# A streaming encoder layer: the third weight tile of attention requested sooner and cast later, other score tiles turned in gate banks, and the convolution behind the next sums

## The chip, the cores and the metric

The kernel runs on one core of a Trainium2 chip. The time is that of the device for one execution, in microseconds. PE multiplies matrices, ACT, DVE and POOL work elementwise, SP and POOL issue DMAs. Each engine runs its own row of instructions in order and waits for semaphores of the others.

## The reference

One layer over 1024 prompt rows and 32 sample rows of width 1024, in float32:

```
h = RMSNorm(x);  z = h @ W_in -> q_A, k_A, v_A, q_B, f_B, i_B, og_B, gate_A, gate_B
y_A = sliding-window attention (16 query heads, 2 kv heads of width 64, sinks, shared relative bias)
y_B = gated linear recurrence (8 heads), RMSNorm(o) * silu(og_B)
m = sigmoid(gate_A) * (y_A @ W_brA) + sigmoid(gate_B) * (y_B @ W_brB)
x = x + RMSNorm(m @ W_out)
[a | u] = RMSNorm(x) @ W_up;  a = causal depthwise conv3(a)
x = x + RMSNorm((gelu(a) * u) @ W_down)
x = x + (p @ W_ple) * sigmoid(x @ W_ple_gate)
```

A frame attends to its own chunk of 64 frames and the two before it.

## The kernel before, in words

**Products.** A float32 operand is split in two parts, a rounded high part and the rest, and a product is three matmuls: with `La`, `Lb` the high part and the rest of the input: `La` by `wh` (L203), `Lb` by `wh` (L204), `La` by `wl` (L205). A weight tile of 512 KB goes through three steps. `load_raw` asks for it (DMA at L173, on SP's queue) into one of two `wr` buffers. `load_next` casts it to the high part `wh` on ACT (L182), and DVE subtracts for the rest `wl` (L184). The plan of tiles is a list; `stream` takes one tile after the other, and keeps tiles ahead up to `limit[0]`.

**Attention.** The stage goes over eight head pairs i (two heads side by side). For each there are nine score tiles j: eight of 128 rows, and j = 8 with the 32 sample rows. `scores(i, j)` multiplies queries by keys (L498, L499), adds bias on DVE (L504), exponentiates on ACT (L509) and scales. `turn(i, j)` transposes the probabilities on PE (L535) into a PSUM bank, and splits them for the next product: ACT casts `ph` (L226), DVE subtracts for `pl` (L227). `values` multiplies them by the values (L554, L555) into a bank `o`, copied on ACT to `u` (L561) and added up on DVE to `ya` (L562, L563); the values of j = 8 go to the third quarter of its own turn's bank.

**What runs between them.** PE is filled with blocks of the projections: queries of the next pair and gates. `stream` counts half-blocks, m = 0, 1, 2 and so on, and `small[m]` lists what is put in behind half-block m: scores, turns, values, weight loads, bias loads. Gate and query blocks write `mm` banks, of which there are three; turns write `tr` banks, of which there are two, or in some cases an `mm` bank. A scheduler orders each engine's row by priority and readiness as it models them; `pinned(f, engines)` and `behind(engines)` hold an instruction behind the last one put on these engines so far. The reading of a finished gate block is a tanh on ACT (L295) and a store on SP (L296). `bias_load` and `bias_load8` fetch the bias of a pair and of its sample tile (L449, L460).

**The up projection.** For each unit f of 128 of the 2816 features, PE runs steps of 24 matmuls into banks X, Y and Z (L2001 to L2003), a scheme of block products from sums of operands. What comes out is combined behind the steps: s1 is copied on ACT (L2012), U2 = s1 - Y on DVE (L2014), L2016 writes a part of `ab`, nU3 = Y - s1 is L2019, L2021 and L2023 write the other factor `us`. L2014 and L2019 are the last readers of the bank Y, so a later step into Y waits for them. `ff_tail(f)` is a generator that runs in unit f + 1: copies at the ends of `ab` (L1937 to L1940), the convolution as one ACT instruction (L1941) and two multiply-adds on DVE (L1942, L1945), the gelu on ACT (L1946) and the product with `us` on DVE (L1947, L1948). Beside it weights are prepared from loaded tiles `wu`: POOL adds tiles (L1759, L1760, L1761, L1766), ACT casts (L1752) and DVE subtracts (L1753).

Of the kernel before, what the change touches and what calls it, by code (L numbers as in the profile page):

```python
# [14 lines left out]
ALU = mybir.AluOpType  # L15
# [44 lines left out]
def layer_kernel(  # L60
# [17 lines left out]
    def nm(s):  # L78
        n_names[0] += 1
        return f"{s}_{n_names[0]}"  # L80
# [5 lines left out]
    V, S, G, E = nc.vector, nc.scalar, nc.gpsimd, nc.tensor  # L86
# [69 lines left out]
    n_first = len(plan)  # L156
# [10 lines left out]
    limit = [n_first]  # L167
    raws, ready, used = [], [], [0]
# [54 lines left out]
    def split(hi, lo, src, scale=None):  # L223

        if scale is None:
            S.copy(hi, src)  # L226
            V.tensor_tensor(lo, src, hi.bitcast(F32), op=ALU.subtract)  # L227
        else:
            S.mul(hi, src, scale)
            V.scalar_tensor_tensor(lo, src, scale, hi.bitcast(F32), op0=ALU.mult, op1=ALU.subtract)  # L230

    def bank(pool, tag, bufs):
        return pool.tile([P, 512], F32, tag=tag, name=nm(tag), bufs=bufs)
# [4 lines left out]
    def mm_bank():  # L238
        return bank(pp, "mm", 3)

    def tr_bank():
        return bank(pp, "tr", 2)
# [35 lines left out]
    def unit(out):  # L278

        cell = []  # L280

        def get_w():
            if not cell:
                cell.append(next_w())
            return cell[0]
        return [(get_w, g, out) for g in range(3)]
# [28 lines left out]
    with right("ap") as ap:  # L315
# [125 lines left out]
        def bias_load(i):  # L441

            bias = aq.tile([P, 2, 256], F32, tag="bias", name=nm("bias"), bufs=2)
            for h in range(2):

                row = rb_d[2 * i + h]
                src = bass.AP(tensor=row.tensor, offset=row.offset + 127,
                              ap=[[368, 8], [383, 16], [1, 256]])
                dma(bias[:, h, :], src)  # L449
            G.memset(bias[0:64, :, 192:256], BIG)  # L450
            G.memset(bias[64:128, :, 0:64], BIG)
            biases[i] = bias

        def bias_load8(i):
            bias8 = aq.tile([64, 160], F32, tag="bias8", name=nm("bias8"), bufs=1)
            for h in range(2):
                row = rb_d[2 * i + h]
                src = bass.AP(tensor=row.tensor, offset=row.offset + 127,
                              ap=[[368, 2], [383, 16], [1, 160]])
                dma(bias8[32 * h:32 * h + 32, :], src)  # L460
            biases[i, 8] = bias8
            yas[i] = aq.tile([P, T], F32, tag="ya", name=nm("ya"), bufs=2)

        def span(j):

            if j == 8:
                return 32, 1024, 160, 0, ((8, 0, P), (9, P, 32))
            if j == 0:
                return P, 0, P, P, ((0, P, P),)
            return P, (j - 1) * P, 256, 0, ((j - 1, 0, P), (j, P, P))  # L470
# [48 lines left out]
        def turn(i, j):  # L519
            m_, k0, nk, b0, tl = span(j)  # L520
            sc = probs.get((i, j))
            ph = aq.tile([P, 2, 2 * P], F32R, tag="ph", name=nm("ph"), bufs=4)
            pl = aq.tile([P, 2, 2 * P], F32R, tag="pl", name=nm("pl"), bufs=4)
            t = mm_bank() if j in (2, 6) else tr_bank()
            n = 2 * len(tl) * m_
            ph, pl = (x[:].rearrange("p a b -> p (a b)")[:, :n] for x in (ph, pl))
            if j == 8:
                for a in range(2):
                    E.transpose(t[:, a * P:(a + 1) * P], sc8[:, a * P:(a + 1) * P], ident[:])
                split(*(x.rearrange("p (a b) -> p a b", b=64) for x in (ph, pl)),  # L530
                      t[:, 0:2 * P].rearrange("p (a b) -> p a b", b=P)[:, :, :64])
            else:
                for a, (_, kc, _) in enumerate(tl):
                    for h in range(2):
                        E.transpose(t[:, (2 * a + h) * P:(2 * a + h + 1) * P], sc[:, h, kc:kc + P],  # L535
                                    ident[:])
                split(ph, pl, t[:, :n])
            probs[i, j] = (ph, pl)
            if j == 8:
                o8[i] = t[:, 2 * P:3 * P]  # L540
# [48 lines left out]
        def pinned(f, *engines):  # L589
            with behind(*engines):  # L590
                f()
# [333 lines left out]
        blocks, small = [(lambda w=w: w, 2, out) for w, out in zip(ws, outs)], {}  # L925
        H_AT = (1, 2, 4, 5)
        of_gates = [b for n in range(N_A) for b in unit(gate_out(GATES[n][0]))]
        for i in range(8):
            lo_ = 2 * len(blocks) if i else 0
            q = unit(q_out(i + 1)) if i < 7 else []  # L930
            g = [of_gates.pop(0) for _ in range(G_AT[i])]
            blocks += g + q if i == 0 else q + g
            hi_ = 2 * len(blocks) - (4 if i == 7 else 0)
            if i == 2:
                small.setdefault(lo_ + 3, []).append(lambda: pinned(bounds, V))
            if i == 0:
                rows_at = [lambda n=n: v_rows[n]() for n in range(9)] + [cache_parts]
                rows_at += [lambda n=n: k_rows[n]() for n in range(2)]
                for m, f in zip((0, 0, 1, *range(2, 20)), rows_at):
                    on = (E, S, V) if f is cache_parts else (E,)  # L940
                    small.setdefault(m, []).append(lambda f=f, on=on: pinned(f, *on))
                for m in (1, 3):
                    small.setdefault(m, []).append(lambda: pinned(load_next, S, V))
                small.setdefault(28, []).append(lambda: lo_by.__setitem__(0, "dma"))
            small.setdefault(lo_ + (4 if i < 7 else 0), []).insert(0, lambda i=i: bias_load8(i))
            if i < 7:
                small.setdefault(lo_ + 2, []).insert(0, lambda i=i: bias_load(i + 1))
            if i in H_AT:
                sums = h_sums(H_AT.index(i))
                next(sums)  # L950
                for m in range(4):
                    small.setdefault(lo_ + 2 * m + 1, []).append(
                        lambda sums=sums: pinned(lambda: next(sums), V))
            for j in range(9):
                at = lo_ + (hi_ - lo_) * j // 9
                if i == 0 and j < 2:
                    small.setdefault(3, []).append(lambda j=j: pinned(lambda: scores(0, j), V))
                else:
                    small.setdefault(at, []).append(lambda i=i, j=j: scores(i, j))
                small.setdefault(at + 3, []).append(lambda i=i, j=j: turn(i, j))  # L960
                if j % 2 or j == 8:
                    js = (8,) if j == 8 else (j - 1, j)
                    small.setdefault(at + (5 if j == 8 else 5), []).append(lambda i=i, js=js: values(i, js))
# [96 lines left out]
    small = {2 * n: [lambda n=n: pinned(lambda: b_prepare(n), V)] for n in range(3)}  # L1060
# [14 lines left out]
    with right("bp") as bp:  # L1075
# [309 lines left out]
        pieces, small = [], {}  # L1385
# [53 lines left out]
        u, v = (unit(gate_out(dst)) for dst, _ in GATES[14:])  # L1439
# [27 lines left out]
    with right("mp") as mp:  # L1467
        Ra = [columns8(rp, 2 * g, "Ra") for g in range(4)]
        Rb = [columns8(rp, 2 * g + 1, "Rb") for g in range(4)]
        small = {}  # L1470
# [98 lines left out]
    rbT = fo.tile([P, T], F32, name="rbT")  # L1569
# [299 lines left out]
    t = tr_bank()  # L1869
# [61 lines left out]
    def ff_tail(f, ab, u):  # L1931

        w0, w1, w2 = (cvec[:, j * NF + f:j * NF + f + 1] for j in range(3))
        bc = cvec[:, 3 * NF + f:3 * NF + f + 1]
        n = T + 2
        a = fp.tile([P, T + 2], F32, tag="a", name=nm("a"), bufs=2)
        V.tensor_copy(tails[:, 0, :, f], ab[:, 1024:1026])  # L1937
        V.tensor_copy(tails[:, 1, :, f], ab[:, 1058:1060])
        with behind(V):
            V.tensor_copy(ab[:, 1026:1028], cach[:].rearrange("p (j f) -> p j f", j=2)[:, :, f])  # L1940
        S.activation(a[:], ab[:, 0:n], AF.Identity, scale=w0, bias=bc)  # L1941
        V.scalar_tensor_tensor(a[:], ab[:, 1:1 + n], w1, a[:], op0=ALU.mult, op1=ALU.add)  # L1942
        V.tensor_tensor(u, u, rbT[:], op=ALU.mult)
        yield
        V.scalar_tensor_tensor(a[:], ab[:, 2:2 + n], w2, a[:], op0=ALU.mult, op1=ALU.add)  # L1945
        S.activation(a[:], a[:], AF.Gelu_apprx_tanh)  # L1946
        V.tensor_tensor(u[:, 0:1024], a[:, 0:1024], u[:, 0:1024], op=ALU.mult)  # L1947
        V.tensor_tensor(u[:, 1024:T], a[:, 1026:1058], u[:, 1024:T], op=ALU.mult)  # L1948
        dma(act_d[f][:], u)
        yield  # L1950
# [212 lines left out]
    for g in range(3):  # L2163
        for q in range(2):
            bs = [mm_bank() for _ in range(4)]
            for k in range(0, NF, 2):
                i = k // 6
# [19 lines left out]
    for s, dst in ((0, o_pconv), (1, o_sconv)):  # L2187
        b = tr_bank()
        E.transpose(b[:44, 0:P], tails[:, s].rearrange("p j f -> p (j f)"), ident[:])
        t = ep.tile([44, P], F32, tag="t", name=nm("tl"), bufs=6)  # L2190
# [97 lines left out]
```

## Time and profile before

| | |
|---|---|
| three runs | 1988.22, 1989.38, 1989.52 us (median 1989.38) |
| profiled execution | 1987.53 us |
| its span in the profile | 1985.8 us |
| mean granted clock of TensorE | 0.999 |
| PE busy | 1963.5 us (99%) |
| DVE, ACT, POOL busy | 1386.5 (70%), 1003.3 (51%), 261.2 us (13%) |
| attention in the trace | from about 58 to 352 us |
| up units 1 to 3 in the trace | from about 1197 to 1260 us |

Durations and start times are of the one profiled execution, in us from the start of its span. In a row of a timeline the first number is the start, the second the duration, then engine, line, operation, output and inputs; brackets at the end give the idle time ahead of it and what ended it. In the list of waits the numbers are the total, the count and the longest. Rows with x2 or x4 stand for several instructions in succession.

### The profile page before, as it was taken

To read this page: it belongs to the slowest core of one execution; us is meant where nothing else is said; L and a number is where in the kernel's file an instruction comes from. 1 tells how busy PE (TensorE), PEld (TensorE's weight loads), DVE (VectorE), ACT (ScalarE), POOL (GpSimd) and SP (SyncE) were. 2 spreads that over 40 slices of the span, in tenths; PEclk is the share of its full clock that TensorE was granted. 3 is DMA by queue.
4 is the path that set the end of the run, shared out by engine and by line. 5 is a ranking of instruction groups with operands and counts; after the bars stand their busy time and mean duration, and the time that the engine had idled before them with its cause. 6 is when DMAs were issued, how large, how long until landed. Compare 5 with 4: busy or idle time off the path is not lost.

```text
span 1985.8 us, 37202 instructions
## 1 busy us (share of the span) xinstructions
PE 1963.5 (99%) x14239; PEld 1948.6 (98%) x14239; DVE 1386.5 (70%) x3059; ACT 1003.3 (51%) x2188; POOL 261.2 (13%) x391
## 2 busy tenths in 40 slices
PE   8999999999999999999999999999999999999998
PEld 8899999999999999999999999999999999999998
DVE  6677777788888888654555878777777784655552
ACT  7567767666656666542225663333333344444332
POOL 2111110000000000002001123334333300000000
PEclk9999999999999999999999999999999999999999
DMA  8533432411122111487558572222222245654542
GB/s 264 144 104 98 124 110 67 132 47 57 56 76 62 55 54 53 128 241 221 181 159 288 194 249 86 69 92 67 83 79 77 86 149 199 215 196 168 164 134 78
DMA packets 255256, 253.57 MB, mean 128 GB/s; under 512 B 14133, under 2 KB 221992, under 8 KB 255077
## 3 DMA queue, kind: packets, MB, share of 16 engines
q1 hardware_dynamic: 244917, 218.43, 35.2%
q0 software_dynamic: 10080, 32.73, 5.4%
q8 instruction: 112, 1.84, 0.4%
q14 instruction: 67, 0.55, 0.1%
q10 hardware_dynamic: 80, 0.03, 0.0%
HBM read 177.89 MB, written 65.32 MB: 122 GB/s over the span
## 4 chain that ended last, share of the span: by engine, by line
PE 89%; DVE 5%; ACT 3%; issue 2%; DMA 1%; POOL 0%; SPq 0%; ACTq 0%; POOLq 0%; DVEq 0%
PE mm L203 13%; PE mm L204 13%; PE mm L205 13%; PE st L2003 7%; PE st L2002 7%; PE st L2001 7%; PE G L1110 2%; PE Y L1107 2%; PE G L1109 2%; PE Y L1110 2%; PE Y L1109 2%; PE G L1107 2%; PE Z L1107 1%; PE Z L1109 1%; PE Z L1110 1%
## 5 line engine op out<-in xcount | busy, mean ns | idle before, releaser
L2001 PE MATMUL st<-op,wt 128*128 128x264 f32 x1232 | 348.7, 283 | 2.5 <-DVE Sp L2014 1.1
L2003 PE MATMUL st<-op,wt 128*128 128x264 f32 x1232 | 349.8, 284 | 0.0
L2002 PE MATMUL st<-op,wt 128*128 128x264 f32 x1232 | 347.6, 282 | 0.0
L2001 PEld LDWEIGHTS st<-op,wt 128*128 128x128 f32 x1232 | 231.2, 188 | 3.8 <-DVE Sp L2014 1.3
L2002 PEld LDWEIGHTS st<-op,wt 128*128 128x128 f32 x1232 | 231.4, 188 | 0.0
L2003 PEld LDWEIGHTS st<-op,wt 128*128 128x128 f32 x1232 | 230.9, 187 | 0.0
L182 ACT CAST wh<-wr 128x1024 fp32r<-128x1024 f32 x125 | 131.1, 1049 | 190.8 <-PE mm L204 136.0
L184 DVE TENSOR_TENSOR wl<-wr,wh 128x1024 fp32r<-128x1024 f32 x114 | 139.6, 1224 | 114.9 <-ACT wh L182 105.7
L1752 ACT CAST wt<-wu 128x512 fp32r<-128x512 f32 x126 | 77.8, 618 | 186.3 <-POOL ab L1987 91.9
L203 PE MATMUL mm<-ac,wh 128*128 128x352 f32 x528 | 170.7, 323 | 0.0
L204 PE MATMUL mm<-ac,wh 128*128 128x352 f32 x528 | 169.1, 320 | 0.0
L205 PE MATMUL mm<-ac,wl 128*128 128x352 f32 x528 | 169.1, 320 | 0.0
L203 PE MATMUL mm<-La,wh 128*128 128x384 f32 (+1 forms) x480 | 158.7, 331 | 0.0
L204 PE MATMUL mm<-Lb,wh 128*128 128x384 f32 (+1 forms) x480 | 155.8, 325 | 0.7 <-DVE Lb L773 0.7
L205 PE MATMUL mm<-La,wl 128*128 128x384 f32 (+1 forms) x480 | 155.5, 324 | 0.2 <-DVE wl L748 0.2
L203 PE MATMUL mm<-Ra,wh 128*128 128x264 f32 x512 | 145.4, 284 | 0.0
L204 PE MATMUL mm<-Rb,wh 128*128 128x264 f32 x512 | 145.0, 283 | 0.0
L205 PE MATMUL mm<-Ra,wl 128*128 128x264 f32 x512 | 145.0, 283 | 0.0
L1753 DVE TENSOR_TENSOR wt<-wu,wt 128x512 fp32r<-128x512 f32 x126 | 103.1, 820 | 50.4 <-ACT wt L1752 50.4
L204 PEld LDWEIGHTS mm<-ac,wh 128*128 128x128 f32 x528 | 99.3, 188 | 0.0
L203 PEld LDWEIGHTS mm<-ac,wh 128*128 128x128 f32 x528 | 99.0, 188 | 0.0
L205 PEld LDWEIGHTS mm<-ac,wl 128*128 128x128 f32 x528 | 98.9, 187 | 0.0
(552 smaller groups left out, 5753.2 us busy)
## 6 DMA issues: line engine op xcount, KB each, us to landing
wr<-in_w_down_dram SPq DMA_DIRECT2D x66, 512.0 KB
wu<-in_w_up_dram SPq DMA_DIRECT2D x42, 512.0 KB
wu<-in_w_in_dram SPq DMA_DIRECT2D x36, 512.0 KB
ac<-act_d SPq DMA_DIRECT2D x66, 176.0 KB
act_d<-Up SPq DMA_DIRECT2D x21, 528.0 KB
wr<-in_w_in_dram SPq DMA_DIRECT2D x21, 512.0 KB
wr<-in_w_out_dram SPq DMA_DIRECT2D x16, 512.0 KB
wl<-wr POOLq DMA_DIRECT2D x11, 512.0 KB, 4.9
```

What stands on the lines that cost most here:

```text
L182: S.copy(hi[:], raw[:])
L184: V.tensor_tensor(lo[:], raw[:], hi[:].bitcast(F32), op=ALU.subtract)
L203: E.matmul(ps, wh, a, start=first and n == 0, stop=False)
L204: E.matmul(ps, wh, b, start=False, stop=False)
L205: E.matmul(ps, wl, a, start=False, stop=last and n == len(ks) - 1)
L1107: E.matmul(o, wh, x[0][k], start=first and k == 0, stop=False, skip_group_check=True)
L1109: E.matmul(o, wh, x[1][k], start=False, stop=False, skip_group_check=True)
L1110: E.matmul(o, wl, x[0][k], start=False, stop=k == 3, skip_group_check=True)
L1753: V.tensor_tensor(t[:, 1], src, t[:, 0].bitcast(F32), op=ALU.subtract)
L2001: E.matmul(o, wh, xh, start=first and k == 0, stop=False, skip_group_check=True)
L2002: E.matmul(o, wh, xl, start=False, stop=False, skip_group_check=True)
L2003: E.matmul(o, wl, xh, start=False, stop=k == 3, skip_group_check=True)
```

## The change

Three edits.

1. In head pair 0 the third and fourth weight tiles of the stage's plan are requested behind half-blocks 3 and 5, and `limit` is set to the tiles that are ready, so that `stream` prepares no other by itself. The third tile's cast and subtraction are put in behind half-block 11, and the limit is set back there. The bias loads of pair 0's last tile and of pair 1 move from half-blocks 4 and 2 to 6 and 8.
2. `turn` takes an `mm` bank for j = 4 and 7, where it was j = 2 and 6.
3. In `ff_tail`, for f < 3, the product of u comes ahead of the first multiply-add, and the generator yields there. The multiply-add is so put on DVE's row later, behind the next unit's L2014.

```diff
@@ turn
-            t = mm_bank() if j in (2, 6) else tr_bank()
+            t = mm_bank() if j in (4, 7) else tr_bank()
@@ attention's lists
                 for m in (1, 3):
                     small.setdefault(m, []).append(lambda: pinned(load_next, S, V))
+                small[3] += [load_raw, lambda: limit.__setitem__(0, len(ready))]
+                small.setdefault(5, []).append(load_raw)
+                small.setdefault(11, []).append(lambda: pinned(load_next, S, V))
+                small[11].append(lambda: limit.__setitem__(0, n_first))
                 small.setdefault(28, []).append(lambda: lo_by.__setitem__(0, "dma"))
-            small.setdefault(lo_ + (4 if i < 7 else 0), []).insert(0, lambda i=i: bias_load8(i))
+            small.setdefault(lo_ + (6 if i < 1 else 4 if i < 7 else 0), []).insert(0, lambda i=i: bias_load8(i))
             if i < 7:
-                small.setdefault(lo_ + 2, []).insert(0, lambda i=i: bias_load(i + 1))
+                small.setdefault(lo_ + (2 if i else 8), []).insert(0, lambda i=i: bias_load(i + 1))
@@ ff_tail
         S.activation(a[:], ab[:, 0:n], AF.Identity, scale=w0, bias=bc)
+        if f < 3:
+            V.tensor_tensor(u, u, rbT[:], op=ALU.mult)
+            yield
         V.scalar_tensor_tensor(a[:], ab[:, 1:1 + n], w1, a[:], op0=ALU.mult, op1=ALU.add)
-        V.tensor_tensor(u, u, rbT[:], op=ALU.mult)
-        yield
+        if f > 2:
+            V.tensor_tensor(u, u, rbT[:], op=ALU.mult)
+            yield
         V.scalar_tensor_tensor(a[:], ab[:, 2:2 + n], w2, a[:], op0=ALU.mult, op1=ALU.add)
```

How it moves instructions. First ACT's row in head pair 0, before; the numbers at the names only tell tiles apart, and the first row is the exponentials of score tile 2:

```order
L509 ACTIVATE sc_1057,st_1058<-sc_1057,st_1058 128x257 x2
L182 CAST wh_1069<-wr_1067 128x1024
L226 CAST ph_1043<-tr_1045 128x512
L345 CAST Vs<-tr_1086 128x2x64
L226 CAST ph_1153<-mm_1155 128x512
L182 CAST wh_1256<-wr_1254 128x1024
L385 COPY vr_1090<-tr_1086 128x128
L345 CAST Vs<-tr_1108 32x2x64
```

The same place after:

```order
L509 ACTIVATE sc_1052,st_1053<-sc_1052,st_1053 128x257 x2
L226 CAST ph_1038<-tr_1040 128x512
L345 CAST Vs<-tr_1079 128x2x64
L385 COPY vr_1083<-tr_1079 128x128
L345 CAST Vs<-tr_1101 32x2x64
L509 ACTIVATE sc_1165,st_1166<-sc_1165,st_1166 128x257
L561 COPY u_1115<-o_1108 128x512
```

The two casts L182 of weight tiles have gone from here, and the split L226 of the second score tile follows the exponentials at once; the turn of tile 2, which was read from an `mm` bank here, comes later and from a `tr` bank.

Next DVE's row in up unit 1, before; `st` is a bank of sums, `Sp` holds s1, U2 and nU3, `a` is the convolution's output:

```order
L1753 TENSOR_TENSOR wt_15293<-wu_15130,wt_15293 128x512
L1942 SCALAR_TENSOR_TENSOR a_15168<-ab_14892,cvec,a_15168 128x1058
L2014 TENSOR_TENSOR Sp_14888<-Sp_14888,st_15177 128x528
L1945 SCALAR_TENSOR_TENSOR a_15168<-ab_14892,cvec,a_15168 128x1058
L1753 TENSOR_TENSOR wt_15324<-wu_15130,wt_15324 128x512
L2016 TENSOR_TENSOR ab_15179<-st_15176,rbT 128x2x264
L1947 TENSOR_TENSOR us_14887<-a_15168,us_14887 128x1024
L1948 TENSOR_TENSOR us_14887<-a_15168,us_14887 128x32
L1753 TENSOR_TENSOR wt_15352<-wu_15130,wt_15352 128x512
L2019 TENSOR_TENSOR Sp_14888<-st_15177,Sp_14888 128x528
```

And after, where the same lines have other numbers (L1757 was L1753, L2022 was L2014, L1949 and L1953 were L1942 and L1945, L2024 was L2016, L1955 and L1956 were L1947 and L1948, L2027 was L2019):

```order
L1757 TENSOR_TENSOR wt_15293<-wu_15130,wt_15293 128x512
L2022 TENSOR_TENSOR Sp_14888<-Sp_14888,st_15176 128x528
L1949 SCALAR_TENSOR_TENSOR a_15168<-ab_14892,cvec,a_15168 128x1058
L1757 TENSOR_TENSOR wt_15324<-wu_15130,wt_15324 128x512
L1953 SCALAR_TENSOR_TENSOR a_15168<-ab_14892,cvec,a_15168 128x1058
L2024 TENSOR_TENSOR ab_15178<-st_15175,rbT 128x2x264
L1757 TENSOR_TENSOR wt_15352<-wu_15130,wt_15352 128x512
L1955 TENSOR_TENSOR us_14887<-a_15168,us_14887 128x1024
L1956 TENSOR_TENSOR us_14887<-a_15168,us_14887 128x32
L2027 TENSOR_TENSOR Sp_14888<-st_15176,Sp_14888 128x528
```

The first multiply-add has moved behind U2, the second behind a weight split, and the weight split that releases POOL's L1766 (now L1770) stands ahead of the product with `us` instead of behind it.

Last PE's row in head pair 7, before, from the turn of j = 0 on; `tr` and `mm` are the banks, `s` the scores of j = 7:

```order
L535 MATMUL tr_4592<-ident,sc_4418 128x128 x2
L535 MATMUL mm_4608<-ident,sc_4448 128x128 x4
L203 MATMUL mm_4639<-La_177,wh_3922 128x384
L204 MATMUL mm_4639<-Lb_181,wh_3922 128x384
L205 MATMUL mm_4639<-La_177,wl_3923 128x384
L203 MATMUL mm_4639<-La_177,wh_3922 128x384
L204 MATMUL mm_4639<-Lb_181,wh_3922 128x384
L498 MATMUL s_4615<-K_1_187,qa_4137 128x256
```

And after, from the same turn on:

```order
L535 MATMUL tr_4592<-ident,sc_4418 128x128 x2
L203 MATMUL mm_4639<-La_177,wh_3922 128x384
L204 MATMUL mm_4639<-Lb_181,wh_3922 128x384
L205 MATMUL mm_4639<-La_177,wl_3923 128x384
L203 MATMUL mm_4639<-La_177,wh_3922 128x384
L204 MATMUL mm_4639<-Lb_181,wh_3922 128x384
L205 MATMUL mm_4639<-La_177,wl_3923 128x384
L203 MATMUL mm_4639<-La_177,wh_3922 128x384
L204 MATMUL mm_4639<-Lb_181,wh_3922 128x384
L498 MATMUL s_4615<-K_1_187,qa_4137 128x256
L535 MATMUL tr_4599<-ident,sc_4433 128x128 x4
L535 MATMUL tr_4608<-ident,sc_4448 128x128 x4
```

The turn of j = 2 no longer stands directly behind that of j = 0 in an `mm` bank, but behind that of j = 1, and both write `tr` banks.

## Prediction

> **What bounds the kernel now.** I read the shares of the page first, then PE's waits, then the windows and timelines around the longest of them.
>
> ```profile
> PE 1963.5 (99%) x14239; PEld 1948.6 (98%) x14239; DVE 1386.5 (70%) x3059; ACT 1003.3 (51%) x2188; POOL 261.2 (13%) x391
> ...
> PE tr L535 <- ACT qb L419: 3.2, 5, 0.7
> PE o L554 <- ACT ph L226: 3.0, 1, 3.0
> ```
>
> PE is busy for 1963.5 of 1985.8 us, and the diff leaves its arithmetic alone. What the change can win is therefore PE's idle time and any stretch in which PE runs at a lower clock. Two rows of the list of waits lie where it edits: five turns of score tiles that wait 3.2 us together, and one product of values that waits 3.0. A third wait, 1.07 us in one step of the up projection, is shown with edit 3.
>
> The longest wait, in the timeline of head pair 0:
>
> ```profile
> 70.18 0.60 PE L535 MATMUL tr<-ident,sc 128*128 128x128 f32 x4
> 70.09 0.20 ACT L509 ACTIVATION_READ_ACCUMULATOR sc<-sc,st 128x1 f32 x1
> 73.49 1.04 ACT L182 CAST wh<-wr 128x1024 fp32r<-128x1024 f32 x1 [3.20 <-DMA wr<-in_w_in_dram]
> 74.44 0.58 ACT L226 CAST ph<-tr 128x512 fp32r<-128x512 f32 x1
> 75.07 0.38 PE L554 MATMUL o<-ph,Vs 128*128 128x256 f32 x1 [2.98 <-ACT ph L226]
> ```
>
> The score tile was turned by 70.78, and ACT had nothing to do from 70.29. But the next instruction in ACT's row was the cast of a weight tile still in flight, so the split that the values need (L226) began only at 74.44, and PE stood 2.98 us.
>
> The windows of the same place show a second price (columns: us, then the busy share of PE, PEld, DVE, ACT and POOL, then PE's granted clock, DMA share, GB/s):
>
> ```profile
> 75.00:76.00 1.00, 0.93 (x6) 0.93 (x7) 1.00 (x2) 1.00 (x4) 0.00 (x0) 1.00 0.05 17
> 76.00:77.00 1.00, 1.00 (x7) 0.82 (x6) 1.00 (x3) 0.89 (x2) 0.00 (x0) 0.71 0.05 14
> 77.00:78.00 1.00, 1.00 (x6) 1.00 (x6) 0.71 (x3) 0.42 (x2) 0.00 (x0) 0.50 0.74 205
> 78.00:79.00 1.00, 1.00 (x5) 1.00 (x4) 0.69 (x4) 0.97 (x5) 0.00 (x0) 0.50 1.13 338
> 79.00:80.00 1.00, 1.00 (x5) 0.90 (x5) 0.91 (x4) 0.95 (x4) 0.00 (x0) 0.58 0.21 50
> 80.00:81.00 1.00, 1.00 (x10) 1.00 (x9) 0.96 (x4) 1.00 (x5) 0.00 (x0) 1.00 0.00 0
> ```
>
> PE is full, but its clock is 0.71, 0.50, 0.50 and 0.58 in four successive microseconds: 0.29 + 0.50 + 0.50 + 0.42 = 1.71 us of work not done. It begins 1.4 us after the stall.
>
> **Edit 1, the weight tile.** The cast and its subtraction leave the places in front of the split, and go to half-block 11, behind the next split. The split can start at 70.8 and end at 71.4; PE reaches the values at 72.1, so the 2.98 go. With them, I take it, goes the slow clock, as no other idle stretch of that size is near: 1.71 more (bounds 0 and 1.71). The two requests now pass the bias loads on SP's queue; those serve pair 0's last score tile and the second pair, many half-blocks later, and their delay costs nothing.
>
> What the moved casts delay is the next candidate. Two casts (1.04 each) and two subtractions (1.23) now fall between these rows:
>
> ```profile
> 84.17 1.04 ACT L182 CAST wh<-wr 128x1024 fp32r<-128x1024 f32 x1
> ...
> 85.25 1.23 DVE L184 TENSOR_TENSOR wl<-wr,wh 128x1024 fp32r<-128x1024 f32 x1 [1.47 <-ACT wh L182]
> ...
> 88.53 0.49 ACT L295 ACTIVATE gt<-mm 128x384 f32<-128x384 f32 x1 [2.34 <-issue]
> ...
> 90.05 0.42 DVE L562 TENSOR_TENSOR ya<-o,u 64x256 f32<-64x256 f32 x1 [2.39 <-ACT u L561]
> ```
>
> One cast and subtraction stand there already, the fifth tile's; the third tile's take their place and the fourth tile's fill idle time of 2.34 us on ACT and 2.39 on DVE. I cost them at 0. Edit 1: -2.98 - 1.71 = **-4.7** (bounds -3.0 and -4.7).
>
> **Edit 2, the banks.** The five waits of 3.2 us look like its prey. Their rows for head pair 2:
>
> ```profile
> 157.46 0.19 DVE L563 TENSOR_TENSOR ya<-tr,u 64x32 f32<-64x32 f32 x1
> ...
> 157.80 0.41 PE L535 MATMUL tr<-ident,sc 128*128 128x128 f32 x2 [0.56 <-ACT qb L419]
> ```
>
> The view blames ACT, but the turn writes a transpose bank, and DVE L563 is the last reader of the tile that held it, the values of the pair before. It ends 0.15 us before the turn starts. That tile is j = 8's; behind it come j = 0 and j = 1, all in the two transpose banks before and after, so j = 1 inherits the same bank from the same reader. These five stay: 0.
>
> Where a turn moves into a transpose bank (j = 2 and 6), it now waits for the reader of the tile two before. In pairs 1 to 6 that reader is done long ahead. In pair 0 (j = 2 behind cache transposes whose readers queue on ACT) and in pair 7, where PE turns j = 1 and j = 2 back to back, I expect a new wait. No row shows it; the nearest, a turn held by DVE, is the 0.56 above. Bounds 0 and 0.56 each, I take 0.35. Edit 2: **+0.7** (0 to 1.1).
>
> **Edit 3, the convolution.** It takes the first multiply-add (L1942) out from in front of the difference L2014. The timeline of unit 1:
>
> ```profile
> 1199.49 1.84 POOL L1760 TENSOR_TENSOR wu<-wu,wu 128x512 f32<-128x512 f32 x1
> ...
> 1199.50 2.99 DVE L1753 TENSOR_TENSOR wt<-wu,wt 128x512 fp32r<-128x512 f32 x3
> ...
> 1202.41 1.31 DVE L1942 SCALAR_TENSOR_TENSOR a<-ab,cvec,a 128x1058 f32<-128x1058 f32 x1
> 1202.63 2.22 POOL L1761 TENSOR_TENSOR wu<-wu,sa 128x512 f32<-128x512 f32 x1 [1.30 <-DVE wt L1753]
> 1203.64 0.69 DVE L2014 TENSOR_TENSOR Sp<-Sp,st 128x528 f32<-128x528 f32 x1
> ...
> 1204.39 0.39 PE L2001 MATMUL st<-op,wt 128*128 128x264 f32 x1 [1.07 <-DVE Sp L2014]
> ...
> 1206.00 1.09 ACT L1946 ACTIVATE a<-a 128x1058 f32<-128x1058 f32 x1 [0.50 <-DVE a L1945]
> 1206.49 0.69 DVE L2016 TENSOR_TENSOR ab<-st,rbT 128x528 f32<-128x528 f32 x1
> 1207.13 1.23 DVE L1947 TENSOR_TENSOR us<-a,us 128x1024 f32<-128x1024 f32 x1
> 1208.27 0.18 DVE L1948 TENSOR_TENSOR us<-a,us 128x32 f32<-128x32 f32 x1
> 1208.37 0.69 DVE L1753 TENSOR_TENSOR wt<-wu,wt 128x512 fp32r<-128x512 f32 x1
> 1208.98 0.70 DVE L2019 TENSOR_TENSOR Sp<-st,Sp 128x528 f32<-128x528 f32 x1
> 1209.20 1.29 POOL L1766 TENSOR_TENSOR wu<-wu 128x512 f32<-128x512 f32 x1 [3.02 <-DVE wt L1753]
> 1209.59 1.45 DVE L1753 TENSOR_TENSOR wt<-wu,wt 128x512 fp32r<-128x512 f32 x1
> 1210.31 0.28 PE L2001 MATMUL st<-op,wt 128*128 128x264 f32 x1
> ```
>
> L2014 moves to 1202.41 and ends at 1203.1, before PE needs it: -1.07. But the same rows show DVE and POOL shutting each other out when both work from SBUF: L1753 takes 0.69 alone and 1.45 beside L1766, L1761 takes 2.22 beside L1942 where L1766 alone takes 1.29, and L1760 (1.84) got in between three L1753 (2.99 instead of 2.07). In the new order L1753 stands ahead of L1947, so it releases L1766 earlier, into the middle of L1947, L1948 and L2019. And L2019 has a deadline: the next step on PE overwrites the bank that it reads, at 1210.31, of which 1.07 was delay, so 1209.24 now.
>
> My walk: L1942 is issued at 1203.0 behind L1761, which ends at 1203.9; L1942 1.31, to 1205.2; L1753 0.69, to 1205.8; L1945 as L1942, to 1207.0; L2016 0.69 and L1753 0.69 bring DVE to 1208.25, the gelu of 1.09 ends at 1208.2. L1947 runs to 1209.4. L1766, released at 1208.4, follows it to 1210.7; L1948 waits for that, and L2019 ends at 1211.4. PE would wait 2.2 us, and behind L2019 only a weight split and L2021 queue, which PE needs a step later. Were L1948 to slip in ahead of L1766, L2019 would end at 1210.15 and PE wait 0.9. I take 2.2, as L1760 did get in between two L1753. The Trainium skill ("SBUF — State Buffer", Who interferes with whom) says that a VectorE instruction with two SBUF inputs and a GpSimd one that reads SBUF exclude each other for the whole instruction, and that issue order decides who goes first; by that rule L1766, which asks a microsecond before L1948, wins as well.
>
> Units 2 and 3, from unit 2's rows:
>
> ```profile
> 1219.27 1.29 POOL L1759 TENSOR_TENSOR sa<-wu 128x512 f32<-128x512 f32 x1 [8.78 <-PE st L2003]
> ...
> 1222.20 0.70 DVE L2014 TENSOR_TENSOR Sp<-Sp,st 128x528 f32<-128x528 f32 x1 [0.52 <-PE st L2003]
> ...
> 1230.65 0.28 PE L2001 MATMUL st<-op,wt 128*128 128x264 f32 x1
> ```
>
> Here L2014 waits for PE until 1222.20, and L1942 now waits behind it. POOL, free of L1942, runs three times 1.3 from 1219.27 to 1223.3. L1942 then ends at 1224.6, L1945 at 1226.4, L1753 at 1227.65, L1947 at 1228.85, L1766 at 1230.1, L2019 at 1230.85, 0.2 after PE's wish. Twice 0.2. Edit 3: -1.07 + 2.2 + 0.4 = **+1.5** (bounds -1.07 and +2.0).
>
> **Sum.** -4.7 + 0.7 + 1.5 = -2.5 us. The profiled execution took 1987.53 us (span 1985.8 and 1.7 around it), so it would take 1985.0. It lies 1.85 below the median of the other three runs, 1989.38 (1988.22 to 1989.52). As four executions spread over 2 us, I start from their mean, 1988.7, and predict **1986.2**. A difference of 0.2%, 4.0 us, is about what a measurement of this kernel can tell from none.
>
> **Rivals.**
>
> *The convolution pays.* L1948 goes before L1766, or the gelu is early enough that L2019 meets its deadline, and the banks cost nothing. Then edit 3 is -0.1 to -1.07, and the sum -4.8 to -5.8: 1982.9 to 1983.9. For it: the walk rests on the one microsecond between L1766's request and L1948's. Against: L1760's row. Chance 0.33, faster.
>
> *The slow clock stays.* If those 1.71 us belong to something else than the stall, the sum is -0.8, time 1987.9. Against: the clock reads 1.00 in the windows on either side. For it: the Trainium skill ("TensorE: Matmul & The Clock Gate", Part 1: The HAM clock gate) halves PE's clock after at least one idle window of a free-running 3.4 us. By that rule a stall of 2.98 us can't fill a window and wouldn't be the cause. Here a stall of 2.98 was followed by a half clock. Chance 0.10, within 0.2%.
>
> *The wait moves to the fifth weight tile.* Its request now stands behind the third tile's subtraction (86.5) and its cast ahead of the softmax of a later score tile. The first pair of requests landed 4.1 us after their issue:
>
> ```profile
> 69.37 1.02 SPq L173 DMA_DIRECT2D wr<-in_w_in_dram x2
> ...
> 92.12 0.52 ACT L509 ACTIVATE sc<-sc,st 128x257 f32<-128x257 f32 x1 [1.62 <-DVE st L504]
> ```
>
> That makes 90.7, a cast to 91.7, and the softmax is wanted at 92.1. If the landing is 3 us later, PE stalls some 2.6 again and loses the clock's 1.7: sum +1.8, 1990.5. Chance 0.07, within 0.2%.
>
> *Slower: the convolution stalls PE long enough to lose the clock.* If POOL gets in twice in each of units 1 to 3 (before L1947 and before L1948), PE waits 2.2 us in each, and if such a wait halves the clock as the 2.98 did, each costs 1.7 more: -4.7 + 0.7 - 1.07 + 3 x 3.9 = +6.6, 1995.3. It decides from a stall somewhere between 1.07, which left the clock alone, and 2.98. Chance 0.08, slower.
>
> *The bank edit does what its place suggests,* and the five waits go: 3.2 less, 1983.0. Against it stands DVE L563. Chance 0.03, faster.
>
> My forecast keeps 0.39, of which 0.03 falls beyond 4 us of gain. Faster 0.33 + 0.03 + 0.03 = 0.39; slower 0.08; same 0.53. The range takes in the first rival (1982.9, less 0.5 for the spread) and reaches half way to the moved wait: 1982.4 to 1989.8.
>
> **What would show it.** In the profile after: no idle row at L554 near 72 us and a clock of 1.00 in all windows from 70 to 85; five waits of 0.6 at the turn of j = 1 still there; in unit 1 no wait for L2014 but one of about 2 us for L2019, with POOL's L1766 between L1947 and L1948; in units 2 and 3 waits of at most 0.3. The forecast is wrong if the clock still falls to 0.5, if a cast of a weight tile again waits for its DMA with PE idle, or if the new L2019 wait is absent or repeats in all three units.

## The result: 3.2 us faster, a wait of 3.0 us gone in attention, and 1.9 us of waiting in place of 1.1 in the up projection

| | before | after |
|---|---|---|
| median of 22 runs each | 1988.3 us (1986.11 to 1990.1) | 1985.07 us (1983.12 to 1986.72) |
| ratio, 95% interval | | 0.9985 (0.9978 to 0.9991) |
| span of the profiled execution | 1985.8 us | 1982.1 us |

That is 0.15%, inside the 0.2% within which the forecast put it, and 1.1 us below the 1986.2 forecast. 0.4 us of the 1.1 come from the start: the 22 runs of before have a median 0.4 below the 1988.7 taken for them. The interval keeps the gain clear of no change.

The list of PE's waits after, as total, count and longest:

```profile
PE tr L535 <- ACT qb L419: 3.4, 5, 0.8
...
PE st L2009 <- DVE Sp L2027: 2.1, 2, 1.9
```

The 3.0 us at the values (L554) and the 1.1 us behind L2014 (now L2022) are off the list. The five turns still wait, and a wait for L2027 (before: L2019) of 1.9 us is new.

Head pair 0 in the timeline:

```profile
69.59 0.60 PE L535 MATMUL tr<-ident,sc 128*128 128x128 f32 x4
70.23 0.59 ACT L226 CAST ph<-tr 128x512 fp32r<-128x512 f32 x1 [0.52 <-PE tr L535]
70.87 0.39 PE L554 MATMUL o<-ph,Vs 128*128 128x256 f32 x1
```

And the windows where the clock had been at 0.71 and 0.50 (busy shares, then PE's granted clock, DMA share and GB/s):

```profile
76.00:77.00 1.00, 1.00 (x10) 0.86 (x9) 0.96 (x4) 0.91 (x5) 0.00 (x0) 1.00 0.00 0
77.00:78.00 1.00, 1.00 (x10) 1.00 (x9) 0.86 (x5) 0.24 (x1) 0.00 (x0) 1.00 0.61 213
```

The split follows the turn at once, PE takes the values with no idle time, and PE keeps a clock of 1.00.

Unit 1 of the up projection, where DVE and POOL do everything in the order that the walk had:

```profile
1197.47 0.69 DVE L2022 TENSOR_TENSOR Sp<-Sp,st 128x528 f32<-128x528 f32 x1
1198.09 2.01 DVE L1949 SCALAR_TENSOR_TENSOR a<-ab,cvec,a 128x1058 f32<-128x1058 f32 x1
...
1203.09 1.22 DVE L1955 TENSOR_TENSOR us<-a,us 128x1024 f32<-128x1024 f32 x1
1203.29 2.14 POOL L1770 TENSOR_TENSOR wu<-wu 128x512 f32<-128x512 f32 x1 [1.14 <-DVE wt L1757]
1204.23 1.26 DVE L1956 TENSOR_TENSOR us<-a,us 128x32 f32<-128x32 f32 x1
1205.41 0.69 DVE L2027 TENSOR_TENSOR Sp<-st,Sp 128x528 f32<-128x528 f32 x1
1206.16 0.39 PE L2009 MATMUL st<-op,wt 128*128 128x264 f32 x1 [1.87 <-DVE Sp L2027]
```

U2 (L2022) ends before PE wants its bank. But a product of 32 columns takes 1.26 us instead of 0.18, since POOL's addition (L1770, before L1766) got in between the two products, and nU3 (L2027) queues behind it. 1.07 us are gone, 1.87 have come.

### The profile page after: what moved, and what is told of

It is laid out like the page before. It is cut to its first block, busy times and chain, and to the rows that moved or that the text cites. A ratio compares the mean times of both kernels' runs of the same rounds, so it can differ in the third digit from the quotient of the medians.

```text
span 1982.1 us, 37207 instructions
## 1 busy us (share of the span) xinstructions
PE 1962.2 (99%) x14239; PEld 1947.3 (98%) x14239; DVE 1387.5 (70%) x3059; ACT 1003.5 (51%) x2188; POOL 258.2 (13%) x391
## 3 DMA queue, kind: packets, MB, share of 16 engines
q8 instruction: 112, 1.84, 0.4%
## 4 chain that ended last, share of the span: by engine, by line
PE 90%; DVE 4%; ACT 2%; issue 2%; DMA 1%; POOL 0%; SPq 0%; DVEq 0%; ACTq 0%; POOLq 0%
PE mm L203 13%; PE mm L205 13%; PE mm L204 13%; PE st L2011 7%; PE st L2010 7%; PE st L2009 7%; PE G L1114 2%; PE Y L1111 2%; PE G L1113 2%; PE Y L1114 2%; PE G L1111 2%; PE Y L1113 2%; PE Z L1111 1%; PE Z L1113 1%; PE Z L1114 1%
## 5 line engine op out<-in xcount | busy, mean ns | idle before, releaser
L182 ACT CAST wh<-wr 128x1024 fp32r<-128x1024 f32 x125 | 131.2, 1050 | 188.4 <-PE mm L204 146.2
L1757 DVE TENSOR_TENSOR wt<-wu,wt 128x512 fp32r<-128x512 f32 x126 | 100.9, 803 | 47.1 <-ACT wt L1756 47.0
```

The costliest lines, as they stand in the source:

```text
L182: S.copy(hi[:], raw[:])
L1757: V.tensor_tensor(t[:, 1], src, t[:, 0].bitcast(F32), op=ALU.subtract)
```

## The experiments

**Each edit alone.** The first three kernels are the kernel before with one edit each, exactly the lines of the diff above: the weight tile with the bias loads; `j in (4, 7)`; the order in `ff_tail`. The fourth has the first two.

> Edit 1 alone on the kernel before. Theory (the edits add up, each acting at its own place): the 2.98 us wait at L554 in head pair 0 and the half clock behind it go, all windows from 70 to 85 us at clock 1.00, the five turns of j = 1 still wait some 0.6 each, L2014 in unit 1 still holds PE for 1.07; 4.0 to 4.7 us faster than before (ratio 0.9976 to 0.9980). Rival (the edits need each other: with the third score tile still turned in a gate bank, a wait of 0.5 to 1 us comes back in pair 0): 3.0 to 3.5 us faster.

Measured: 1983.58 us, ratio to before 0.9978 (0.9969 to 0.9988), 4.4 us faster. No wait at the values in pair 0, clock 1.00 from 69 to 82 us; L2018 (L2014 before) holds PE for 1.0. The edit does its work alone, whether the third score tile is turned in a gate bank (`mm`) or not.

> Edit 2 alone on the kernel before. Theory: the five waits at the turn of j = 1 stay (3.2 us in all), the 2.98 us in pair 0 stays with its half clock, nothing new over 0.3 us in pair 7; no difference (within 0.7 us). Rival, as the prediction sized it: new waits in pairs 0 and 7, 0.7 us slower. Other rival: the five waits go, 3 us faster.

Measured: 1989.5 us, ratio 1.0003 (0.9994 to 1.0012): no difference. The waits of this kernel:

```profile
PE tr L535 <- ACT qb L419: 3.1, 5, 0.7
PE o L554 <- ACT ph L226: 2.9, 1, 2.9
```

The five stay, as was foreseen from DVE's L563. One thing was not expected. The stall in its timeline, and the windows behind it:

```profile
74.77 0.38 PE L554 MATMUL o<-ph,Vs 128*128 128x256 f32 x1 [2.87 <-ACT ph L226]
```

```profile
76.00:77.00 1.00, 1.00 (x10) 0.92 (x9) 1.00 (x5) 0.52 (x2) 0.00 (x0) 1.00 0.18 51
77.00:78.00 1.00, 1.00 (x8) 0.82 (x7) 0.59 (x4) 0.93 (x4) 0.00 (x0) 1.00 0.91 262
78.00:79.00 1.00, 1.00 (x9) 1.00 (x10) 0.96 (x4) 0.96 (x5) 0.27 (x1) 1.00 0.91 270
```

A stall of 2.87 us, at the place where 2.98 had halved the clock, left it at 1.00. So the 1.71 us are not lost in every execution; the last experiments are about this. The theory had kept the half clock, and was wrong there.

> Edit 3 alone on the kernel before. Theory (the wait moves within unit 1): the 1.07 us for L2014 goes and about 1.9 us for L2019's successor comes, with the short product (128x32) taking 1.26 instead of 0.18 behind POOL; 0.8 us slower. Rival (the 1.9 us only appear together with the other edits' shift in time): 1.07 us faster. The clock stays at 1.00 in the windows behind the 1.9 us.

Measured: 1989.1 us, ratio 1.0011 (1.0002 to 1.002), 2.2 us slower by the ratio, 0.4 to 4.0 by its interval. The wait of 1.87 us comes without the other edits, and in this trace the clock stays at 1.00 behind it. From the list of waits:

```profile
PE o L554 <- ACT ph L226: 2.5, 1, 2.5
...
PE st L2005 <- DVE Sp L2023: 2.1, 2, 1.9
```

> The change without edit 3. Theory: as edit 1 alone, 4.0 to 4.7 us faster than before and 0.8 us faster than the whole change; the wait of 1.07 us for L2014 in unit 1 is back, that of 1.9 us is gone. Rival: no faster than the whole change (3.2 us faster than before).

Measured: 1983.43 us, ratio 0.9979 (0.997 to 0.9988), 4.2 us faster than before. Its median lies 1.6 below the whole change; the two intervals overlap, so the difference rests on the two traces: 1.06 us for L2018 here, 1.87 for L2027 there. So edit 3, as it was made, costs time.

**What makes nU3 late.** The changed kernel with two lines exchanged:

```diff
+        V.tensor_tensor(u[:, 1024:T], a[:, 1026:1058], u[:, 1024:T], op=ALU.mult)
         V.tensor_tensor(u[:, 0:1024], a[:, 0:1024], u[:, 0:1024], op=ALU.mult)
-        V.tensor_tensor(u[:, 1024:T], a[:, 1026:1058], u[:, 1024:T], op=ALU.mult)
```

> The changed kernel with the two products of the convolution's tail exchanged: the short one (128x32) before the long one (128x1024). Theory (POOL's addition takes the memory port behind the long product and shuts out the short one, and with it the nU3 difference queued behind): now nothing that POOL can shut out stands between the long product and nU3, the short product takes 0.18 again, the 1.87 us wait in unit 1 falls to about 0.8; 1.1 us faster than the changed kernel, 4.3 faster than before (ratio 0.9978). Rival (nU3 is late because more instructions stand ahead of it): the wait stays at 1.9 us, and the time at 3.2 faster than before.

Measured: 1982.68 us, ratio to before 0.9973 (0.9964 to 0.9983), 5.4 us faster by the ratio. In its timeline L1955 is now the short product and L1956 the long one:

```profile
1202.40 0.19 DVE L1955 TENSOR_TENSOR us<-a,us 128x32 f32<-128x32 f32 x1
1202.51 1.22 DVE L1956 TENSOR_TENSOR us<-a,us 128x1024 f32<-128x1024 f32 x1
1202.60 2.25 POOL L1770 TENSOR_TENSOR wu<-wu 128x512 f32<-128x512 f32 x1 [1.14 <-DVE wt L1757]
...
1203.64 0.70 DVE L2027 TENSOR_TENSOR Sp<-st,Sp 128x528 f32<-128x528 f32 x1
1204.26 1.15 DVE L1757 TENSOR_TENSOR wt<-wu,wt 128x512 fp32r<-128x512 f32 x1
1204.40 0.39 PE L2009 MATMUL st<-op,wt 128*128 128x264 f32 x1 [0.80 <-DVE Sp L2027]
```

The same work stands ahead of nU3, and the wait is 0.80 instead of 1.87. POOL's addition still comes behind the long product, but what it shuts out now is a weight split behind nU3 (1.15 instead of 0.68), and nU3 itself, which reads a PSUM bank (`st`), runs beside it in its usual 0.70. The rival by mere order falls: the short product's place behind POOL's addition is what cost 1.07 us.

The products behind nU3, by a third yield in `ff_tail` that is consumed after `after(3, ps)` in units 1 to 3:

```diff
         S.activation(a[:], a[:], AF.Gelu_apprx_tanh)
+        if f < 3:
+            yield
         V.tensor_tensor(u[:, 0:1024], a[:, 0:1024], u[:, 0:1024], op=ALU.mult)
```

> The changed kernel with the tail's two products put behind nU3 in units 1 to 3 (one more yield behind the gelu). Theory (the wait in unit 1 is nU3 standing behind the products and POOL): nU3 ends before PE wants its bank, both the 1.07 us and the 1.87 us waits are gone, nothing over 0.3 us in units 1 to 3; 1.9 us faster than the changed kernel, 5.1 faster than before (ratio 0.9974), the fastest of all. Rival (the wait moves on, to the subtraction of the weights or to the factor us, which stand behind the products now): 0.5 to 1 us of a new wait at a later step of unit 1.

Measured: 1983.08 us, ratio 0.9974 (0.9964 to 0.9983). Unit 1 has no wait of either kind any more; unit 2 has one of 0.48 behind the copy of s1, so part of the rival holds. With the exchange of two lines it is the fastest here, 2 us below the change; the two can't be told apart, nor can either from the change without edit 3 (0.9979).

**Which half of the weight edit.** The kernel before with the requests sooner (and the bias loads later), but the cast left to the scheduler:

```diff
                 for m in (1, 3):
                     small.setdefault(m, []).append(lambda: pinned(load_next, S, V))
+                small[3] += [load_raw]
+                small.setdefault(5, []).append(load_raw)
```

> Half of edit 1 on the kernel before: the two weight tiles are requested sooner, ahead of the bias loads, but cast where the scheduler puts them, and the limit is left alone. Theory (what PE waits for is the tile's landing, some 4 us behind its request): requested at 66.6 instead of 69.4 us it lands near 70.7, the wait at L554 shrinks to 1 to 2 us and the clock stays at 1.00; 2.5 to 3.5 us faster than before. Rival (the cast's place on ACT is what counts): the exponentials and the split stand behind the cast, a wait over 2.5 us and a half clock remain, under 1 us faster.

Measured: 1984.73 us, ratio 0.9985 (0.9977 to 0.9994), 3 us faster than before. The request came sooner than expected, at 64.7, and the wait is a little shorter than the 1 to 2 us expected:

```profile
64.70 1.19 SPq L173 DMA_DIRECT2D wr<-in_w_in_dram x2
...
68.98 1.05 ACT L182 CAST wh<-wr 128x1024 fp32r<-128x1024 f32 x1 [0.92 <-DMA wr<-in_w_in_dram]
70.93 0.56 ACT L226 CAST ph<-tr 128x512 fp32r<-128x512 f32 x1
71.55 0.38 PE L554 MATMUL o<-ph,Vs 128*128 128x256 f32 x1 [0.89 <-ACT ph L226]
```

The cast starts 4.3 us behind the request (4.1 before); asked for sooner, it leaves a wait of 0.89. The rest is the cast's place: it still stands ahead of two exponentials and the split. So the sooner request takes 2.1 of the 2.98 us and the later cast the last 0.9.

**When the clock falls.** DVE is held up in the changed kernel, ahead of nU3, in units 4 to 20, by maxima of a tile with itself that change no value. PE then stands at later steps, mostly for s1. In the first kernel the sizes go round, in the others they rise in every second unit:

```diff
             elif i == 3:
+                if u >= 4:
+                    ...
+                        V.tensor_tensor(rbT[:, 0:k], rbT[:, 0:k], rbT[:, 0:k], op=ALU.max)
                 V.tensor_tensor(nU3[:, sl], y, s1c[:, sl], op=ALU.subtract)
```

> The changed kernel with DVE held up ahead of nU3 in units 4 to 20 by maxima of a tile with itself, of four sizes in turn (2456, 2965, 3304 and 3812 elements a row), so that PE stands some 2.0, 2.6, 3.0 and 3.6 us, four or five times each. Theory (a stall over some limit between 1.87 and 2.54 us halves the clock for 3.4 us, whatever it coincides with): clock 1.00 behind the five of 2.0, 0.5 behind all twelve others, 1.7 us lost behind each. Rival (only a stall that fills a 3.4 us window does): 1.00 behind all of 3.0 and less. Other rival (it depends on where in a fixed grid of windows the stall falls): 0.5 behind some stalls of each size and not behind others.

Measured: 2021.13 us in one execution. The stalls came fewer and shorter than aimed at: eight of the 17 held units have one, of 1.8 to 3.4 us. Two of them, as the PE rows behind them in the timeline, and two windows behind each:

```profile
1329.07 0.39 PE L2009 MATMUL st<-op,wt 128*128 128x264 f32 x1 [2.19 <-ACT Sp L2020]
...
1372.65 0.39 PE L2009 MATMUL st<-op,wt 128*128 128x264 f32 x1 [1.90 <-ACT Sp L2020]
```

```profile
1330.00:1331.00 1.00, 1.00 (x10) 1.00 (x9) 1.00 (x2) 0.00 (x0) 0.00 (x0) 1.00 0.00 0
1331.00:1332.00 1.00, 1.00 (x11) 1.00 (x10) 1.00 (x2) 0.23 (x1) 0.10 (x1) 1.00 0.00 0
...
1374.00:1375.00 1.00, 1.00 (x7) 1.00 (x6) 1.00 (x2) 0.00 (x0) 0.00 (x0) 0.50 0.00 0
1375.00:1376.00 1.00, 1.00 (x6) 1.00 (x6) 0.92 (x2) 0.65 (x1) 0.10 (x1) 0.50 0.06 16
```

2.19 us left the clock alone and 1.90 halved it: neither the limit by length nor the window that must be full. That leaves the third expectation, though not in its words: no length had both outcomes here. The three stalls of 1.83 to 1.91 us that the hold made all halved the clock, and the four of 2.19 to 2.21 did not. Two more kernels were made for it.

> The changed kernel with DVE held up ahead of nU3 in every second unit from 4 to 20 by maxima of a tile with itself, of 1700 elements a row rising by 150 from one held unit to the next, so that PE stands between about 1 and 3 us at nine places. Theory (a free-running grid of 3.41 us windows; the clock halves for one window when more than about 1.84 us of the window before was idle): every half-clock stretch begins a whole number of 3.41 us from every other, lasts 3.41 us, and follows each stall that has 1.9 us or more within one window, none that has less than 1.8 in each. Rival (the length of the stall decides, whatever its place): one length divides the stalls with from those without.

> The same with 2300 elements in the first held unit, rising by 150: stalls of about 1.5 to 3.5 us at other places of the grid. Theory and rival as before; by the theory a stall of 2 to 2.9 us that a boundary cuts into two parts under 1.8 us leaves the clock at 1.00, while a shorter one inside a window halves it.

Measured: 2014.19 and 2018.7 us, one execution each. In the later of the two, two stalls of the same length with different outcomes, and a window behind each:

```profile
1419.52 0.39 PE L2009 MATMUL st<-op,wt 128*128 128x264 f32 x1 [2.00 <-ACT Sp L2020]
...
1462.69 0.39 PE L2009 MATMUL st<-op,wt 128*128 128x264 f32 x1 [1.99 <-ACT Sp L2020]
```

```profile
1420.00:1421.00 1.00, 1.00 (x11) 1.00 (x10) 1.00 (x3) 0.00 (x0) 0.00 (x0) 1.00 0.00 0
...
1464.00:1465.00 1.00, 1.00 (x6) 1.00 (x6) 1.00 (x2) 0.00 (x0) 0.00 (x0) 0.50 0.00 0
```

Where a slow stretch starts can be worked out from the clocks of the windows: a window of 1 us at 0.74 has 0.52 us at half speed. In each of the three traces the starts lie whole multiples of 3.413 us apart, to 0.01 of one (first kernel 0, 26, 52, 78 and 110 of them; second 0, 47, 60, 73, 86, 100, 113; third 0, 14, 40, 53, 79). So there is a grid, and each stall can be cut where its lines fall. The columns give which of the three kernels, the start of the stall, its length, what of it lies in each window, and the work lost behind it; 11 of the 26 stalls over 1.8 us are shown:

| kernel | stall at | length | idle in the grid's windows | lost behind it |
|---|---|---|---|---|
| first | 1280.51 | 3.42 | 0.35, 3.07 | 1.70 |
| first | 1326.89 | 2.19 | 1.76, 0.43 | 0 |
| first | 1370.75 | 1.90 | 1.90 | 1.71 |
| first | 1548.24 | 1.83 | 1.83 | 1.71 |
| first | 1593.02 | 2.19 | 1.86, 0.33 | 0 |
| second | 1205.30 | 1.87 | 1.87 | 1.71 |
| second | 1543.84 | 3.58 | 1.56, 2.02 | 1.70 |
| third | 1206.21 | 1.86 | 1.41, 0.45 | 0 |
| third | 1417.52 | 2.00 | 1.73, 0.28 | 0 |
| third | 1460.71 | 1.99 | 1.99 | 1.71 |
| third | 1594.15 | 2.17 | 2.17 | 1.70 |

Over all 26, 1.87 us or more of idle time within one window is followed by a halved one (15 times), 1.81 or less isn't, and between them two of 1.83 are and one of 1.86 isn't. Of the 17 slow stretches 16 last one window. One, in the third kernel from 1327.07 on, lasts two: the stall ahead of it, of 3.58 us, left 0.65 idle in the halved window too. In the second kernel 0.59 left so did not prolong the stretch; why, these runs don't tell.

Every other trace can be cut in the same way, since each ends in a slow stretch, when PE has nothing left to do, and steps of 3.4133 us can be counted back from its start. In the trace of before the clock is 0.73 from 1984 to 1985 us and 0.50 behind, so that stretch starts at 1984.46, and 559 steps ahead of it lies 76.42, where the slow stretch of pair 0 starts:

| trace | stall at | length | idle in the grid's windows | lost behind it |
|---|---|---|---|---|
| before | 72.09 | 2.98 | 0.91, 2.07 | 1.71 |
| edit 2 alone | 71.91 | 2.87 | 1.62, 1.25 | 0 |
| edit 3 alone | 70.89 | 2.54 | 0.02, 2.52 | 1.71 |
| edit 3 alone | 1207.10 | 1.87 | 0.45, 1.42 | 0 |
| after | 1204.29 | 1.87 | 0.58, 1.29 | 0 |

All five go as the grid says. So the half clock of before belonged to the stall, and the stall of edit 2 alone kept its clock because a line cut it. The row of the second of the three kernels at 1205.30 is the change's own wait in unit 1: in this execution it cost 1.87 and then 1.71 more. Its timeline row, and the windows:

```profile
1207.17 0.39 PE L2009 MATMUL st<-op,wt 128*128 128x264 f32 x1 [1.87 <-DVE Sp L2034]
```

```profile
1207.00:1208.00 1.00, 0.83 (x5) 0.84 (x6) 1.00 (x3) 0.00 (x0) 0.00 (x0) 0.74 0.66 270
1208.00:1209.00 1.00, 1.00 (x6) 1.00 (x6) 0.93 (x2) 0.04 (x1) 0.00 (x0) 0.50 0.66 270
```

## Why the prediction was right, and which terms were off

**Edit 1 (-4.7, alone -4.4).** The wait went whole, and no wait took its place behind it in pair 0 or at the fifth tile: neither the rival with the slow clock nor the one with the moved wait came. The term that was too sure is the clock's 1.71, taken as lost in every execution because one profile showed it. By the grid, with the border at 1.84 us, an estimate is that a stall of 2.98 at a random place loses it in 79 of 100 cases: when it lies inside one window (0.43 of 3.41), and when a line cuts it and leaves 1.84 on one side (twice 1.14 of 3.41). That makes -2.98 - 1.35 = -4.3. The three traces that have this stall fit, each by its cut: two lost it (2.98, and 2.54 in the kernel with edit 3 alone), one (2.87) didn't.

**Edit 2 (+0.7, alone within noise of 0).** That the five waits would stay was right, and the rows fit the reason given: in the trace after, L563 again ends 0.15 us before the turn starts, here and in the other four. No run moved L563, so that it is what ends these waits is read from the rows, and not shown.

```profile
152.35 0.19 DVE L563 TENSOR_TENSOR ya<-tr,u 64x32 f32<-64x32 f32 x1
...
152.69 0.63 PE L535 MATMUL tr<-ident,sc 128*128 128x128 f32 x4 [0.56 <-ACT qb L419]
```

The 0.35 each for new waits in pairs 0 and 7 was wrong: no turn waits there. The price came from a row of a wait at another place, and the question was whether there would be a wait here at all.

**Edit 3 (+1.5; by the traces +0.8).** U2's wait went (-1.07), POOL got in ahead of the short product, and PE waited for nU3, all as walked: 1.87 against 2.2. Of the 0.33 between them, half comes behind the first multiply-add and half behind POOL's addition, where the two engines take turns. The walk let the one that was shut out start when the other ended and then take its whole time. In the trace after, the first multiply-add (L1949) ends 1.12 us behind POOL's addition of L1765 (1197.69 and 1.29), where it takes 1.31 alone, and POOL's L1770 ends 1.12 behind the long product, where it takes 1.29 alone. For units 2 and 3 the walk had 0.2 each; there the same two gains bring nU3 to its end 0.2 us ahead of PE's wish. The short product is shut out there too (1.27 and 1.28), with no one waiting. Had the short product slipped in ahead, the prediction had PE waiting 0.9; with the two lines exchanged it waits 0.80. What the term lacked is the clock: a wait of 1.87 that falls inside one window costs 1.71 more. Of the five traces with this wait (after, edit 3 alone, and the three with DVE held up later) one lost it.

**The sum.** -2.98 and -1.35 in pair 0, -1.07 + 1.87 in unit 1, and 1.71 in (3.41 - 1.87) / 3.41 = 45 of 100 executions, +0.77: -2.8 (an estimate, as it takes every place in the grid for equally likely). Measured -3.2, with an interval of -1.8 to -4.4. The forecast of -2.5 came so near it by luck, by errors of opposite sign: it counted 0.4 too much of the clock in pair 0, none of the 0.77 in unit 1, and 1.4 us of waits that did not come (0.7 for the banks, 0.3 in unit 1, 0.4 in units 2 and 3).

The mean clocks of all runs fit this. Each is given to 0.001 only, 2 us, so their order says more than their size: 0.9985 before and with edit 2 alone, 0.9983 with edit 3 alone, 0.9996 with edit 1 alone and with edits 1 and 2, 0.9991 with the whole change. That is how it should look if edit 1 takes slow stretches away and edit 3 brings some back.

The rival on the slower side asked whether PE's new waits would lose the clock. They can, in one unit; units 2 and 3 have no such wait, so the clock's price is 0.77 on average by this estimate, and not three times 1.7.

## What to carry to other kernels

An instruction that waits for a transfer should not stand ahead of a short one that PE waits for; asking sooner took some two thirds of this stall (2.1 of 2.98 us), moving the cast the rest. When an operation is moved behind another, look at what it releases: here a weight split released POOL's addition into the middle of DVE's row, and a 32-column product paid 1.08 us; two lines exchanged gave that back. A slow stretch seen in one profile is one draw: find out in how many executions it occurs before its whole length goes into a sum.

## What the runs showed of the hardware

PE's clock is judged in a grid of 3.413 us windows that the program doesn't align: some 1.85 us idle within one window halve the clock for the next (for the next two in one of 17 cases), which costs 1.71 us of a full PE, while 2.87 us that a line cut into 1.62 and 1.25 cost no clock. The Trainium skill ("TensorE: Matmul & The Clock Gate", Part 1: The HAM clock gate) has the free-running window of 3413 ns, and the traces agree to 0.01 of a window. It has the half rate come after at least one idle window; here 1.87 of 3.41 us idle was enough, and the measurement decides. All stalls here were single ones; no run shows what several small waits in one window do.
